# A mixer projection formed from seven block products instead of eight, with its input blocks kept on chip

## The chip, the cores and the metric

The kernel runs on one core of one Trainium2 chip. The metric is device time in microseconds (us), the median of several runs. The engines are named as the profile names them: PE (matrix products; PEld is its weight load), DVE (vector), ACT (scalar), POOL (GpSimd) and SP (which issues most DMAs here). Each engine runs its own instructions in a fixed order and waits at semaphores for the others.

## The reference

One decoder block over 1024 tokens of width 1024, in float32. What matters here is the middle of it:

```python
out_a = glu_a * jax.nn.sigmoid(glu_b)                  # from the state-space branch
out_b = att @ w_fox_o[l]                               # from the attention branch
gate_a, gate_b = jnp.split(jax.nn.sigmoid(gate_logits), 2, axis=-1)
h = h + (gate_a * out_a + gate_b * out_b) @ w_mix_out[l]
h = h + memory_cross_attention(rms_norm(h, norm_mem_q[l]), ..., w_mem_q[l], ...)
f_a, f_b = jnp.split(rms_norm(h, norm_ffn[l]) @ w_ffn_in[l], 2, axis=-1)
h = h + (jax.nn.silu(f_a) * f_b) @ w_ffn_out[l]
```

The mixer projection is the product with `w_mix_out` (1024 x 1024). The block `gate_a * out_a + gate_b * out_b` is called "merged" below.

## The kernel before

Every float32 operand is split into a high part (an fp32r cast, on ACT) and a low part (source minus high part, on DVE or POOL), by `split`. A product of two such operands is three matmuls: high by high, high by low, low by high. One matmul takes a 128 x 128 weight tile and 512 columns.

`stage_tail` holds everything from the gated unit on. Channels go in eight tiles of 128 (index `j`), tokens in eight tiles of 128 (`t`) or two halves of 512 (`h`).

- **The gated unit** (`Glu`): for each `j`, `value` and `sigmoid` form two products of 512 columns; DVE copies the first (L1239), ACT takes the sigmoid of the second into a half-width buffer `sb` (L1244), DVE multiplies them into the tile `sg` (L1245). `gate` then loads the gate `ga` from DRAM and multiplies `sg` by it on POOL (L1252), in two halves. The half-width buffers `sb`, `ga` and `gb` come from one small ring, so a new one waits for an older one's reader.
- **The attention branch** (`fox_part`): `po` is a product with `w_fox_o` (L173 to L175 with `ath`, `atl`) in a PSUM bank "pv" or "misc"; DVE multiplies it by the gate `gb` from DRAM (L616) and adds it to `sg` (L617). The merged tile is then split into `mxh`, `mxl` (`mT`).
- **The mixer** (`mix`): for each token tile and each half of the output, 8 channel tiles x 3 matmuls into one bank, then DVE adds a piece of `x` into `H[t]` (L668). The weights are `mix_weights`. Between the first twelve of these, `weave` puts the steps of `ahead(0)`, `ahead(1)`, `ahead(2)`, which prepare operands of the first three feed-forward tiles (`wpr`, `wph`, `wpl`) and store them to DRAM. The last four are followed by the norms of token tiles 0 to 3 (`norm`: a square on ACT, L190; a power on POOL, L211; small DVE steps L207 to L217; the scaled tile `xs` on DVE, L231; transposes on PE, L237; splits `u2h`, `u2l`).
- **The queries** (`mem_q`): products of `u2` with `w_mem_q`, with the norms of token tiles 4 to 7 between them.

The order on each engine is set by the build: a scheduler places the instructions by its own model within the order of the code, `B.behind(...)` and `issue_after` hold something back behind a named instruction, and pools of buffers (`wpool` with `whi`, `wlo` and four `raw`; `big` with bslot; `s2` with 16 slots; PSUM banks by tag) make a new tile wait for the last reader of an old one.

Of the kernel before, what the change touches and what calls it, by code (L numbers as in the profile page):

```python
# [9 lines left out]
F32 = mybir.dt.float32  # L10
F32R = mybir.dt.float32r
# [107 lines left out]
class Block:  # L119
# [126 lines left out]
    def norm_turn(self, xs, act, t):  # L246

        for b in range(2):
            cast = self.turned(self.turn(xs, b, ("misc", "pv")[b]), b, act, t)
        return cast  # L250
# [331 lines left out]
def stage_tail(B, big, s2, sh, x, glu, aT, gate_d, kv_d, w_fox_o, w_mix_out, g_mq, w_mem_q, w_mem_o, g_ffn,  # L582
# [18 lines left out]
    mT = Act(s2, "t", NS2, 8, L, name="mx")  # L601
    fox = {}

    def fox_part(j):
# [6 lines left out]
        for h in range(2):  # L611
# [5 lines left out]
            V.tensor_add(sg[:, cs], sg[:, cs], gb)  # L617
            mh, ml = mT.rhs(j, h)
            merged.append(B.split(mh, ml, sg[:, cs]))

    merged = []
    for j in range(8):
# [4 lines left out]
        glu.rest(j)  # L627
        if j > 2:
            fox_part(j - 3)
    for j in range(5, 8):  # L630
        fox_part(j)


    H = [bslot(name=f"h{t}") for t in range(NT)]
    gq = B.bcast_gain(s2, g_mq)
    u2 = Act(s2, "t", NS2, 8, L, name="u2")
# [6 lines left out]
    def wslots(src, pool_lo):  # L643

        nk = src.shape[0] // P
        raw = B.wpool.tile([P, RAW], F32, tag="raw", bufs=4, name="raw")[:, :D]
        S.dma_start(raw.rearrange("p (k c) -> p k c", k=nk), src.rearrange("(k p) c -> p k c", p=P))
        hl = bslot(F32R, "wbh"), bslot(F32R, "wbl")
        B.split(*hl, raw, pool_lo)
        return [t_.rearrange("p (k c) -> p k c", k=nk) for t_ in hl]  # L650

    def mix_weights(c):

        wm = ([], [])
        for kk in range(4):
            if c == 0:
                hl = B.wblock(w_mix_out, 2 * kk, 2, 0, 512)
            else:
                hl = wslots(w_mix_out[2 * kk * P:(2 * kk + 2) * P, 512:D], False)
            for w_, t_ in zip(wm, hl):  # L660
                w_ += [t_[:, 0, :], t_[:, 1, :]]
        return wm

    def mix(t, c, wm):
        cs = slice(512 * c, 512 * c + 512)
        ps = B.bank()
        gemm_n(ps, mT, t, wm, 8)
        V.tensor_add(H[t][:, cs], ps, load(x[t * P:(t + 1) * P, cs], "xr"))  # L668

    def norm(t, gb, act):  # L670
        xs = s2.tile([P, D], F32, tag="xs", bufs=1, name="xs")
        B.norm_scale(xs, H[t], B.rstd(H[t]), gb)
        return B.norm_turn(xs, act, t)
# [6 lines left out]
    def ahead(j):  # L680
# [14 lines left out]
        def plain():  # L695
            hl, _ = pair(0)
            with B.behind(merged[-1]):
                B.split(*hl, pre[j][0])
# [38 lines left out]
    with B.behind(merged[-1]):  # L737
        wm1 = mix_weights(1)
# [1252 lines left out]
```

## Time and profile before

| | |
|---|---|
| median of 3 runs | 1540.18 us (1540.08, 1540.18, 1541.64) |
| profiled execution, first to last instruction | 1538.1 us (its own time is not listed apart; the median lies 2.1 us above the span) |
| PE busy | 1520.7 us, 99% of the span, 7329 matmuls |
| DVE, ACT, POOL busy | 1005.7, 658.1, 253.6 us |
| granted PE clock | 0.999 |
| last sigmoid products and attention branch | up to 679.6 us |
| mixer products | 679.8 to 769.6 us |
| queries from | 770.6 us |

Times in the trace count from the span's first instruction. A row of the timeline gives the start, the length, the engine, the line, the operation and its tiles, how many instructions are merged in it, and in brackets the idle time before it with what ended it. A row of the stages gives for each engine its busy time and its number of instructions, then the granted PE clock, the share of the DMA engines that was busy, and their GB/s. A row of the groups gives the count, the busy total, the mean of one in ns, and the idle time before.

### The profile page before, as it was taken

The numbers are of one execution on the slowest core, as the hardware profiler recorded it, in microseconds if no ns is written. First come the engines' busy times: TensorE is split into PE (matmuls) and PEld (weight loads), VectorE is DVE, ScalarE is ACT, GpSimd is POOL, SyncE is SP. The second block draws the span as 40 slices with busy tenths as digits, with TensorE's granted clock in tenths as the row PEclk, the third lists the DMA queues.
The fourth block names the chain that finished last, engine by engine and source line by source line (L and its number), as shares of the span: only waits on it lengthen the run. The fifth ranks groups of instructions, "written<-read, shape, count | busy, mean of one in ns | idle before, by whom it ended". The sixth has DMA issues, their size and how long they took to land. (4 is left out here: it accounts for less than half of the span.)

```text
span 1538.1 us, 20434 instructions
## 1 busy us (share of the span) xinstructions
PE 1520.7 (99%) x7329; PEld 1257.7 (82%) x7329; DVE 1005.7 (65%) x1828; ACT 658.1 (43%) x1183; POOL 253.6 (16%) x341
## 2 busy tenths in 40 slices
PE   8999999999999999999999999999999999999998
PEld 7888888898777678888888888888888888888886
DVE  7936554355878867675556797777777775675555
ACT  7423334324667643232435663333333333354343
POOL 1166542100121214100102200000000000101001
PEclk9999999999999999999999999999999999999999
DMA  9634556611223746378210356555544544896542
GB/s 286 161 104 102 131 128 144 180 41 16 50 46 88 192 131 198 111 218 308 89 69 1 117 204 210 162 161 160 158 158 157 157 145 139 291 391 220 192 163 110
DMA packets 196293, 234.06 MB, mean 152 GB/s; under 512 B 35576, under 2 KB 127656, under 8 KB 195680
## 3 DMA queue, kind: packets, MB, share of 16 engines
q1 hardware_dynamic: 188704, 214.93, 47.0%
q10 hardware_dynamic: 7488, 17.83, 3.1%
q8 instruction: 57, 0.93, 0.3%
q14 instruction: 44, 0.36, 0.1%
HBM read 161.94 MB, written 72.71 MB: 153 GB/s over the span
## 5 line engine op out<-in xcount | busy, mean ns | idle before, releaser
L184 DVE TENSOR_TENSOR wlo<-raw,whi 128x1024 fp32r<-128x1024 f32 (+2 forms) x120 | 126.3, 1058 | 45.4 <-ACT whi L183 44.2
L183 ACT CAST whi<-raw 128x1024 fp32r<-128x1024 f32 (+2 forms) x120 | 108.7, 910 | 105.6 <-PE mm L174 39.1
L184 DVE TENSOR_TENSOR ol<-or,oh 128x1024 fp32r<-128x1024 f32 x73 | 90.1, 1236 | 74.0 <-ACT oh L183 71.9
L173 PE MATMUL mm<-uh,whi 128*128 128x512 f32 x344 | 136.5, 397 | 0.0
L174 PE MATMUL mm<-ul,whi 128*128 128x512 f32 x344 | 135.1, 393 | 0.0
L175 PE MATMUL mm<-uh,wlo 128*128 128x512 f32 x344 | 134.5, 391 | 0.0
L183 ACT CAST oh<-or 128x1024 fp32r<-128x1024 f32 x73 | 76.9, 1054 | 105.0 <-PE mm L1108 34.2
L997 POOL TENSOR_TENSOR g<-a,c 128x512 f32<-128x512 f32 x22 | 35.7, 1621 | 389.0 <-ACT a L996 389.0
L175 PEld LDWEIGHTS mm<-uh,wlo 128*128 128x128 f32 x344 | 64.7, 188 | 13.3 <-DVE wlo L184 0.2
L1803 POOL TENSOR_TENSOR pl<-pf,ph 128x512 fp32r<-128x512 f32 (+1 forms) x32 | 36.8, 1152 | 232.5 <-DVE ph L1802 193.3
L173 PEld LDWEIGHTS mm<-uh,whi 128*128 128x128 f32 x344 | 64.8, 188 | 11.6
L174 PEld LDWEIGHTS mm<-ul,whi 128*128 128x128 f32 x344 | 64.8, 188 | 11.0
L1800 ACT ACTIVATE pf<-sc 128x512 f32<-128x512 f32 (+1 forms) x96 | 46.4, 489 | 44.5 <-DVE sc L1796 28.3
L986 DVE SCALAR_TENSOR_TENSOR c<-c,pv 128x512 f32<-128x512 f32 x22 | 15.1, 687 | 76.5 <-ACT c L985 76.4
L211 POOL TENSOR_TENSOR r<-ms,mhalf 128x1 f32<-128x1 f32 (+1 forms) x26 | 15.7, 605 | 298.6 <-DVE ms L207 258.5
L964 PE MATMUL pv<-S3h,we 128*128 128x512 f32 x176 | 57.7, 389 | 0.0
L1806 DVE TENSOR_TENSOR pl<-pf,ph 128x512 fp32r<-128x512 f32 (+2 forms) x64 | 35.3, 553 | 10.4 <-ACT ph L1805 9.8
L1108 PE MATMUL mm<-ol,oh 128*128 128x512 f32 (+1 forms) x110 | 41.9, 381 | 0.0
L1108 PE MATMUL mm<-oh,ol 128*128 128x512 f32 (+1 forms) x110 | 41.9, 381 | 0.0
L1108 PE MATMUL mm<-oh 128*128 128x512 f32 (+1 forms) x110 | 41.9, 381 | 0.0
L173 PE MATMUL sc<-uh,whi 128*128 128x512 f32 x104 | 40.8, 392 | 0.0
L173 PE MATMUL mm<-yh,whi 128*128 128x512 f32 x104 | 40.7, 392 | 0.0
(639 smaller groups left out, 4554.2 us busy)
## 6 DMA issues: line engine op xcount, KB each, us to landing
or<-c_d SPq DMA_DIRECT2D x77, 256.0 KB
wo<-in_w_ffn_out_dram SPq DMA_DIRECT2D x22, 512.0 KB
c_d<-g SPq DMA_DIRECT2D x44, 256.0 KB
t_d<-wo SPq DMA_DIRECT2D x44, 256.0 KB
or<-t_d SPq DMA_DIRECT2D x44, 256.0 KB
rawb<-in_w_ffn_in_dram SPq DMA_DIRECT2D x20, 512.0 KB
raw<-in_w_ffn_in_dram SPq DMA_DIRECT2D x20, 512.0 KB
raw<-in_w_in_dram SPq DMA_DIRECT2D x19, 512.0 KB
```

Of the source, the lines that this page charges most:

```text
L173: T.matmul(ps, lh, rh, start=first, stop=False)
L174: T.matmul(ps, lh, rl, start=False, stop=False)
L175: return T.matmul(ps, ll, rh, start=False, stop=last)
L183: cast = self.A.copy(hi, src)
L184: self.rest = (self.G if pool_lo else self.V).tensor_sub(lo, src, f32(hi))
L211: self.G.tensor_tensor(out=r, in0=v, in1=self.mhalf[:, 0:n], op=ALU.pow)
L964: T.matmul(ps, l_[:, k, :], r_, start=first and k == 0 and i == 0, stop=k == 3 and i == 2, skip_group_check=True)
L997: G.tensor_mul(g[:, 512:], a1, c1)
L1108: T.matmul(ps, l_[:, gi], r_[:, c0:c1], start=k == 0 and (p == NP - LAST if own else p == 0 and n in (1, 2, 7)), stop=p == NP - 1 and k == ...
L1800: self.exp = A.activation(pf[:, off:], ps[:, off:], AF.Exp)
L1803: G.tensor_sub(pl[:, off:], pf[:, off:], f32(ph[:, off:]))
L1806: self.left = V.tensor_sub(pl[:, off:], pf[:, off:], f32(ph[:, off:]))
```

## The change

The mixer becomes seven products of 512-wide blocks (Winograd's form of Strassen's scheme): 7 products x 4 channel tiles x 4 token tiles x 3 matmuls, in place of 8 x 2 x 8 x 3.

- `fox_part` adds into block tiles (`block(n, p)`, kept on chip: `m1` to `m7`) instead of `sg`, and no longer splits; `merged_pair` makes four block combinations with four DVE instructions for each of four pairs.
- The weight combinations are made among the gated unit's steps: `mix_fetch` loads two weight tiles (`ws1`, `ws2`), `mix_sums` adds four halves on POOL, `mix_store` writes the four results to DRAM (`mt_d`). They are called for pairs 0 to 3 at `j` = 0 to 5.
- `m_get(m)` makes the operands of step `m` (28 steps, order `MORDER`): the weight half is loaded again, from `w_mix_out` or `mt_d`; ACT casts both halves, DVE makes the low part of the block half, POOL that of the weight half. Steps 0 to 3 use `whi`/`wlo`, later ones a ring of four pairs (`moh`, `mol`).
- `m_mm`, `m_step` and `m_add` do the products, in two sets of four banks, and add each finished product to `H`, which is now loaded with `x` first. Product 2 goes token tile by token tile (`m_tile`), product 3 follows; the norms of token tiles 0 to 3 are woven between them, both transposes in "pv" banks.
- `ahead(0)` is woven into steps 2 to 19; the steps of `ahead(1)` and `ahead(2)` are listed after them, among the last mixer steps and the queries; `plain` is no longer held behind the last merged tile.

```diff
-            V.tensor_add(sg[:, cs], sg[:, cs], gb)
-            mh, ml = mT.rhs(j, h)
-            merged.append(B.split(mh, ml, sg[:, cs]))
+            n = ((None, 1), (4, 2))[j % 2][h]
+            dst = block(n, j // 2) if n else sg[:, cs]
+            V.tensor_add(dst, sg[:, cs], gb)
...
+    def merged_pair(p):
+        a21 = gs.pop(p)
+        a11, a12, s1 = block(1, p), block(2, p), block(5, p)
+        V.tensor_sub(block(7, p), a11, a21)
+        V.tensor_sub(s1, block(4, p), a21)
+        V.scalar_tensor_tensor(out=block(6, p), in0=s1, scalar=-1.0, in1=a11, op0=ALU.mult, op1=ALU.subtract)
+        V.scalar_tensor_tensor(out=block(3, p), in0=block(6, p), scalar=-1.0, in1=a12, op0=ALU.mult, op1=ALU.subtract)
...
+    def mix_fetch(p):
+        msum[p] = slot(name="ws1"), slot(name="ws2")
+        for i, t_ in enumerate(msum[p]):
+            S.dma_start(t_, w_mix_out[(2 * p + i) * P:(2 * p + i + 1) * P, :])
+
+    def mix_sums(p):
+        w1, w2 = msum[p]
+        b11, b12, b21, b22 = w1[:, :512], w1[:, 512:], w2[:, :512], w2[:, 512:]
+        for o, i in ((b11, b12), (b12, b22), (b22, b11), (b21, b22)):
+            G.tensor_add(o, o, i)
+
+    def mix_store(p):
+        w1, w2 = msum.pop(p)
+        for n, o in ((5, w1[:, :512]), (7, w1[:, 512:]), (6, w2[:, 512:]), (4, w2[:, :512])):
+            S.dma_start(mt_d[n, p], o)
...
         glu.rest(j)
+        if j < 4:
+            mix_fetch(j)
+        if 0 < j < 5:
+            mix_sums(j - 1)
+        if 1 < j < 6:
+            mix_store(j - 2)
         if j > 2:
             fox_part(j - 3)
...
+    def m_get(m):
+        n, p = mseq[m]
+        rb = B.wpool.tile([P, RAW], F32, tag="raw", bufs=4, name="raw")[:, :512]
...
+        S.dma_start(rb, src)
+        if m < 4:
+            hl = [B.wpool.tile([P, WSLOT], F32R, tag=t_, name=t_)[:, :D] for t_ in ("whi", "wlo")]
+        else:
+            hl = bslot(F32R, "moh"), bslot(F32R, "mol")
+        B.split(hl[0][:, :512], hl[1][:, :512], mblk[n, p])
+        B.split(hl[0][:, 512:], hl[1][:, 512:], rb, True)
+        mops[m] = hl
+
+    def m_mm(m, i, ps):
+        n, p = mseq[m]
+        hi, lo = mops[m]
+        gi = slice(i * P, (i + 1) * P)
+        for k, (l_, r_) in enumerate(((hi, hi), (hi, lo), (lo, hi))):
+            T.matmul(ps, l_[:, gi], r_[:, 512:], start=k == 0 and p == 0 and n in (1, 2, 7),
+                     stop=p == 3 and k == 2, skip_group_check=True)
...
+        set_ = msets[n in (7, 4)]
+        for i in range(4):
+            m_mm(m, i, set_[i])
+        if p == 3:
+            for i in range(4):
+                m_add(n, i, set_[i])
+
+    def m_tile(i):
+        ps = B.bank(("mm", "misc")[i % 2])
+        for p in range(4):
+            m_mm(20 + p, i, ps)
+        m_add(2, i, ps)
...
+    weave([lambda m=m: m_next(m) for m in range(2, 20)], ahead(0), 4)
+    last = [lambda i=i: (m_tile(i), m_next(20 + i)) for i in range(4)] + [lambda m=m: m_step(m) for m in range(24, 28)]
+    fetched, *later = ahead(1) + ahead(2)
+    weave(last, [lambda t=t: norm(t, gq, u2, ("pv", "pv")) for t in range(4)] + [fetched])
```

How the instructions stand now is shown at three places. The first is POOL during the gated unit. `sg` tiles are multiplied by `ga` (the gates of `j` = 2 and 3 have `sg_5863` and `sg_5942`); `ws1`, `ws2` are the new weight sums. Before, the gates follow one another:

```order
L1252 TENSOR_TENSOR sg_5772<-sg_5772,ga_6087 128x512
L1252 TENSOR_TENSOR sg_5772<-sg_5772,ga_6090 128x512
L1252 TENSOR_TENSOR sg_5863<-sg_5863,ga_6125 128x512
L1252 TENSOR_TENSOR sg_5863<-sg_5863,ga_6128 128x512
L1252 TENSOR_TENSOR sg_5942<-sg_5942,ga_6163 128x512
```

Now, behind the gate of `j` = 1, twelve adds stand ahead of and between the gates of `j` = 2 and 3; the first four, of pair 0, stand ahead of these rows:

```order
L654 TENSOR_TENSOR ws1_6082<-ws1_6082 128x512
L654 TENSOR_TENSOR ws1_6082<-ws1_6082,ws2_6083 128x512
L654 TENSOR_TENSOR ws2_6083<-ws2_6083,ws1_6082 128x512
L1341 TENSOR_TENSOR sg_5863<-sg_5863,ga_6122 128x512
L654 TENSOR_TENSOR ws2_6083<-ws2_6083 128x512
L1341 TENSOR_TENSOR sg_5863<-sg_5863,ga_6125 128x512
L654 TENSOR_TENSOR ws1_6128<-ws1_6128 128x512
L654 TENSOR_TENSOR ws1_6128<-ws1_6128,ws2_6129 128x512
L654 TENSOR_TENSOR ws2_6129<-ws2_6129,ws1_6128 128x512
L654 TENSOR_TENSOR ws2_6129<-ws2_6129 128x512
L1341 TENSOR_TENSOR sg_5942<-sg_5942,ga_6172 128x512
```

Between the gates of `j` = 1 and `j` = 3 there were two instructions, the halves of the gate of `j` = 2; now there are fourteen.

The second is SP's queue at the same place, ahead of the first loads of `gb`. Before:

```order
L158 DMA raw_6629<-in_w_fox_o_dram 128x4x256
L222 DMA gbc_6801<-in_norm_mem_q_dram 128x1024
L1251 DMA ga_6163<-gate_d_79 128x512
L1251 DMA ga_6166<-gate_d_79 128x512
L597 DMA gb_6188<-gate_d_79 128x512
```

And now:

```order
L648 DMA ws1_6128<-in_w_mix_out_dram 128x1024
L648 DMA ws2_6129<-in_w_mix_out_dram 128x1024
L659 DMA mt_d_6001<-ws1_6040 128x512 x2
L659 DMA mt_d_6001<-ws2_6041 128x512 x2
L1340 DMA ga_6172<-gate_d_79 128x512
L1340 DMA ga_6175<-gate_d_79 128x512
L648 DMA ws1_6178<-in_w_mix_out_dram 128x1024
L648 DMA ws2_6179<-in_w_mix_out_dram 128x1024
L659 DMA mt_d_6001<-ws1_6082 128x512 x2
L659 DMA mt_d_6001<-ws2_6083 128x512 x2
L597 DMA gb_6209<-gate_d_79 128x512
```

The weight loads and the stores of the sums, which wait for POOL, have moved ahead of the loads that DVE's step L616 (now L617) needs.

The third is DVE at the mixer's end. Before, the last additions to `H` (L668) stand one at a time, each with one norm's steps behind it:

```order
L668 TENSOR_TENSOR h6_6799<-mm_7400,xr_7425 128x512
L184 TENSOR_TENSOR u2l0_0_6811<-misc_7441,u2h0_0_6803 128x2x128
L231 SCALAR_TENSOR_TENSOR xs_7487<-h3_6796,r01_7492,gbc_6801 128x1024
L184 TENSOR_TENSOR u2l1_0_6813<-misc_7441,u2h1_0_6805 128x2x128
L184 TENSOR_TENSOR u2l2_0_6815<-pv_7450,u2h2_0_6807 128x2x128
```

Now the last four (L710, of product 3) stand around the norm of tile 3, and splits of the query weights (`wlo`) behind them:

```order
L710 TENSOR_TENSOR h4_6706<-h4_6706,sc_6846 128x512
L216 SCALAR_TENSOR_TENSOR rt1_7577<-rt1_7577,ms1_7575 128x1
L184 TENSOR_TENSOR u2l3_0_6724<-pv_7538,u2h3_0_6716 128x2x128
L217 SCALAR_TENSOR_TENSOR r01_7576<-rt1_7577,r01_7576 128x1
L710 TENSOR_TENSOR h5_6707<-h5_6707,sc_6847 128x512
L231 SCALAR_TENSOR_TENSOR xs_7571<-h3_6705,r01_7576,gbc_6932 128x1024
L710 TENSOR_TENSOR h6_6708<-h6_6708,mm_6848 128x512
L710 TENSOR_TENSOR h7_6709<-h7_6709,mm_6849 128x512
L184 TENSOR_TENSOR u2l0_0_6718<-pv_7584,u2h0_0_6710 128x2x128
L184 TENSOR_TENSOR wlo_7645<-raw_7642,whi_7644 128x1024
```

`xs_7571`, which PE turns for the queries' operands, now follows two of the additions. The order also shows that the scheduler has put most of `ahead(1)` and `ahead(2)` on ACT and DVE among steps 15 to 20 of the mixer, earlier than the code lists them.

More of the change, by code (lines that the diff above doesn't have):

```diff
@@ L598, in load @@
         return t_
-    mT = Act(s2, "t", NS2, 8, L, name="mx")
-    fox = {}
+    fox, gs, done = {}, {}, {}
+    mt_d = B.dram.tile([8, 4, P, 512], F32, name="mt_d")
+    mblk = {}
     def fox_part(j):
@@ L641, in gemm_n, with norm @@
             B.mm3(ps, ah, al, w[0][k], w[1][k], k == 0, k == nk - 1)
[L643 to L670, printed above, removed]
+    def norm(t, gb, act, banks=("misc", "pv")):
         xs = s2.tile([P, D], F32, tag="xs", bufs=1, name="xs")
         B.norm_scale(xs, H[t], B.rstd(H[t]), gb)
-        return B.norm_turn(xs, act, t)
+        return B.norm_turn(xs, act, t, banks)
     AHEAD_IN = 2
```

77 lines of the change are left out of this document (59 added, 18 removed).

## The prediction

> **What bounds the kernel now.** I read the busy shares first, then the stages around the change, then PE's rows there, then POOL, DVE and SP in the gated unit. The shares (busy us, share, instructions):
>
> ```profile
> PE 1520.7 (99%) x7329; PEld 1257.7 (82%) x7329; DVE 1005.7 (65%) x1828; ACT 658.1 (43%) x1183; POOL 253.6 (16%) x341
> ```
>
> PE is the bound overall. The stages tell whether it also is where the change works:
>
> ```profile
> 590.00:595.00 5.00, 5.00 (x23) 4.14 (x23) 3.25 (x3) 1.75 (x3) 3.64 (x2) 1.00 0.95 282
> 595.00:600.00 5.00, 5.00 (x23) 4.13 (x22) 3.70 (x3) 0.28 (x1) 3.61 (x2) 1.00 0.86 309
> 600.00:605.00 5.00, 5.00 (x23) 4.13 (x22) 1.43 (x3) 0.62 (x1) 2.53 (x2) 1.00 0.85 257
> 679.00:723.00 44.00, 44.00 (x196) 36.44 (x195) 27.69 (x39) 14.74 (x21) 0.00 (x0) 1.00 0.84 278
> 723.00:770.00 47.00, 47.00 (x223) 39.16 (x222) 24.69 (x59) 18.64 (x45) 3.87 (x7) 1.00 0.36 126
> 770.00:802.00 32.00, 31.90 (x159) 26.31 (x158) 15.42 (x33) 11.16 (x28) 0.55 (x1) 1.00 0.22 83
> ```
>
> PE never waits in the mixer (679 to 770), and 0.10 us in the 32 behind it. So each matmul removed is worth its full pitch, and each new wait costs its full length. The reader should also see two things that are nearly full without being the bound: the DMA engines at 590 to 605 (0.85 to 0.95), and that POOL is idle in the mixer today.
>
> **The gain.** PE's rows give the pitch:
>
> ```profile
> 592.77 0.39 PE L173 MATMUL pv<-ath,whi 128*128 128x512 f32 x1
> 609.09 0.39 PE L173 MATMUL misc<-ath,whi 128*128 128x512 f32 x1
> 611.81 0.39 PE L173 MATMUL pv<-ath,whi 128*128 128x512 f32 x1
> ```
>
> From 609.09 to 611.81 are 12 matmuls: 2.72/12 = 0.2267 us each. The mixer had 8 x 2 x 8 x 3 = 384 and has 7 x 4 x 4 x 3 = 336. 48 fewer: **-10.9 us**. The transposes stay the same in number.
>
> **The gated unit.** Here the change adds POOL and DMA work. The rows:
>
> ```profile
> 590.83 3.64 POOL L1252 TENSOR_TENSOR sg<-sg,ga 128x512 f32<-128x512 f32 x2 [5.27 <-DMA ga<-gate_d]
> 596.10 3.61 POOL L1252 TENSOR_TENSOR sg<-sg,ga 128x512 f32<-128x512 f32 x2 [1.64 <-DMA ga<-gate_d]
> 600.13 2.53 POOL L1252 TENSOR_TENSOR sg<-sg,ga 128x512 f32<-128x512 f32 x2 [0.42 <-DMA ga<-gate_d]
> 612.71 3.01 POOL L1252 TENSOR_TENSOR sg<-sg,ga 128x512 f32<-128x512 f32 x2 [10.05 <-DVE sg L1245]
> 590.98 1.15 DVE L1245 TENSOR_TENSOR sg<-sg,sb 128x512 f32<-128x512 f32 x1
> 595.32 1.23 DVE L184 TENSOR_TENSOR wlo<-raw,whi 128x1024 fp32r<-128x1024 f32 x1
> 596.46 2.24 DVE L1245 TENSOR_TENSOR sg<-sg,sb 128x512 f32<-128x512 f32 x1
> 612.53 0.68 DVE L616 TENSOR_TENSOR gb<-gb,misc 128x512 f32<-128x512 f32 x1
> 613.25 1.32 DVE L617 TENSOR_TENSOR sg<-sg,gb 128x512 f32<-128x512 f32 x1
> 594.68 0.60 ACT L1244 ACTIVATE sb<-sc 128x512 f32<-128x512 f32 x1
> 587.81 1.07 SPq L1251 DMA_DIRECT2D ga<-gate_d x2
> DMA packets 3431, 4.24 MB, mean 283 GB/s; under 512 B 217, under 2 KB 2247, under 8 KB 3431
> ```
>
> (The last is the DMA view of 590 to 605.) POOL takes 2.53/2 = 1.265 us for a 128x512 operation when DVE is idle, and one beside a DVE instruction with two SBUF operands costs some 1.1 us more a pair (3.64, 3.61); DVE's own goes from 1.15 to 2.24, or from 0.68 to 1.32. A DVE instruction that reads PSUM (L616) stays at 0.68.
>
> The chain in the new order: `fox_part(1)`'s second half takes the "pv" bank that DVE frees by `gb x po` of `fox_part(0)`. On DVE that multiplication now stands behind the last sigmoid multiplication of `j` = 4, whose `sb` buffer is the `ga` that POOL reads in the first gate half of `j` = 3. Ahead of that half POOL has the twelve adds and the gate of `j` = 2: 15 operations counting itself, from 594.47 (590.83 + 3.64) on.
> - POOL: 15 x 1.265 = 19.0, to 613.5; five DVE instructions with two SBUF operands fall there, I count four at 1.08: to 617.8.
> - Then the sigmoid 0.60, the DVE multiplication beside POOL 2.24, `gb x po` 0.68: 621.3.
> - PE reaches that product at 611.81 + 6 x 0.2267 (six matmuls of the next product have been put ahead) = 613.2. **Wait 8.1 us.**
>
> Bounds: with no meeting 613.5 + 0.60 + 1.15 + 0.68 = 615.9, a wait of 2.7; with the cheapest POOL operation of that shape in the trace (below, 1.04) 15.6 us, and no wait: 0. All five meetings and 1 us for late loads give 10.3. I take 8.1, since the nearest rows are gates beside DVE. A second path ends there too: `gb` for that step now stands behind eight `ws` loads (4.2 MB) and eight stores (2.1 MB); with six gate halves, itself and one raw tile that makes 8.4 MB from 587.81 on, at 283 GB/s 29.6 us, to 617.4, and 0.68: a wait of 4.9 even if POOL were fast. Once PE is late, the later gates are in time: by the same prices pair 3's adds and the gate of `j` = 4 end by 630, their product is due at 638.
>
> **The mixer's steps.** Prices:
>
> ```profile
> L184 DVE TENSOR_TENSOR mxl<-sg,mxh 128x512 fp32r<-128x512 f32 x16 | 11.0, 688 | 2.8 <-ACT mxh L183 2.8
> L184 DVE TENSOR_TENSOR wpl<-wpr,wph 128x1024 fp32r<-128x1024 f32 x1 | 1.2, 1219 | 0.0
> 769.77 0.69 DVE L668 TENSOR_TENSOR h<-mm,xr 128x512 f32<-128x512 f32 x1 [1.68 <-PE mm L175]
> ```
>
> The removed `mxh`/`mxl` splits (16 each) and the sixteen pair combinations cancel on DVE; both lie beside PE, and cost nothing there. At step 4 PE needs the first bank read out by an addition that stands behind a 1.22 us split: 0 to 1.9 us, taken 0.7, since the split may have run.
>
> Steps 4 to 19 take PE 16 x 2.72 = 43.5 us, and PE reaches step 23's operands 9 matmuls later, 45.6. In that time DVE has, by the new order, 36 SBUF instructions at 0.688, one at 1.22 and 16 additions at 0.69: 37.0. POOL has 16 x 1.265 = 20.2, one after each step, where it had 0.00 and 3.87 in two stages. One meeting for each POOL operation at 1.32 - 0.69 = 0.63 makes DVE 47.1: **1.5 us late** at `m_tile(0)`. With no meeting 0; with one and a half for each 52.2, 6.6. I take the single meeting, as in the row at 613.25. The 4 MB of raw loads here replace the mixer's weights of like size; the stage 679 to 723 carried 278 GB/s without a wait of PE.
>
> [...]
>
> **The tail.** Norms 0 to 3 and product 3 are packed, and the norms of tiles 4 to 7 start later than before relative to PE:
>
> ```profile
> 764.22 0.63 ACT L190 ACTIVATE junk<-h 128x512 bf16<-128x512 f32 x1
> 766.47 0.20 DVE L207 TENSOR_SCALAR ms<-ss 128x1 f32<-128x1 f32 x1
> 766.75 0.55 POOL L211 TENSOR_TENSOR r<-ms,mhalf 128x1 f32<-128x1 f32 x1 [5.82 <-DVE ms L207]
> 767.75 0.15 DVE L216 SCALAR_TENSOR_TENSOR rt<-rt,ms 128x1 f32<-128x1 f32 x1
> 770.20 0.37 ACT L183 CAST u2h<-misc 128x256 fp32r<-128x256 f32 x1 [3.25 <-PE misc L237]
> 770.95 1.27 DVE L231 SCALAR_TENSOR_TENSOR xs<-h,r,gbc 128x1024 f32<-128x1024 f32 x1
> 772.14 0.42 DVE L184 TENSOR_TENSOR u2l<-misc,u2h 128x256 fp32r<-128x256 f32 x1
> 770.00 0.60 PE L237 MATMUL pv<-ident,xs 128*128 128x128 f32 x4
> ```
>
> - Product 3's first step uses the ring buffers that `m_tile(3)`'s early matmuls free, 10 matmuls (2.3 us) ahead; two casts and POOL's 1.265 need some 3.1 (casts taken as long as a square, 0.63 each, and hops): 0.8.
> - The turn of tile 2 needs, on DVE from `m_tile(2)`'s end on, six additions and low parts (4.1), six `u2l` (2.5), the power 0.55, small steps 0.7 and `xs` 1.27: 9.1 without a gap, against 37 matmuls (8.4) and two turns (1.2). With gaps for casts 0 to 1.4: 0.7.
> - The turn of tile 3 waits for `xs`, which stands behind two additions: 0.69 + 0.69 + 1.27 and hops and small steps 0.7, against the 9 matmuls left, 2.0: 1.3.
> - The turn of tile 4 follows two additions (1.38), four `u2l` (1.68), two `wlo` (2.46), three `ms` (0.60), the power 0.55, small steps 0.5, `xs` 1.27: 8.4, against two turns (1.2) and 28 matmuls (6.3): 0.9.
>
> Together **3.7 us**; 1.5 if the first two are covered by casts done early and the rest by half, 6 if each meets POOL. In the kernel before each addition of 0.69 stood alone, so none of these waits showed at 770 to 802.
>
> **The sum.** -10.9 + 8.1 + 0.7 + 1.5 + 3.7 = +3.1. The profiled span of 1538.1 becomes 1541.2; the median lies 2.1 above the span (1540.18), so **1543.3 us**.
>
> **The rivals.**
> 1. *The gates are not late.* Place: POOL from 594.47 on. If its adds cost what the nearest other 128x512 POOL operation costs, the chain ends before PE comes:
>
> ```profile
> L782 POOL TENSOR_TENSOR pe<-pe,sm x16: 1039/1040/2107, 807.1 to 865.6; 128x512 f32<-128x512 f32 x16
> ```
>
> At 1.04 us the wait is 0 and the time 1543.3 - 8.1 = 1535.2, faster. It turns faster (by 3.1 us) where the wait is below 1.9, so at up to 1.21 us for each operation. Against it: `sm` is spread from a narrower operand, the gates never went under 1.265, and the loads would need 340 GB/s.
>
> 2. *DVE and POOL take full turns in the steps.* Place: steps 4 to 23. Price: 37.0 + 20.2 = 57.2 us less what the additions (which read PSUM) cover, at most 10.1; halfway 52.2, 6.6 late instead of 1.5, and 1.3 more in the gated unit (5.9 us for five meetings in place of 4.3, less the shorter multiplication behind them): 1549.7. It decides once a step loses over 0.54 us ((45.6 - 37.0)/16). For it: the pair at 590.83. Against: the pair at 612.71, and that additions come four in a row. [...]
>
> 3. *The tail is hidden*: the scheduler's spread of the steps suffices, and 3.7 goes: 1539.6. For it: 31.90 of 32 us busy today with the same norms. Against: the order of the additions.
>
> **Chances.** A measurement of this kernel tells about 0.2%, 3.1 us, from no change. The forecast has 0.49: 0.28 slower, 0.21 within, as it lies on that bound. Rival 1 has 0.26 (0.22 faster, 0.04 within), rival 2 0.14 (slower), rival 3 0.11 (0.09 within, 0.02 faster). Faster 0.24, same 0.34, slower 0.42. The forecast's own range is 1538 to 1548; to leave out no more than 0.2 I go to 1533 (rival 1 with a tail of 1.5) and 1551 (past rival 2's time).
>
> **What would show it.** Right: PE waits once for 5 to 10 us near 613, released by DVE's L617, POOL's gates there 8 us or more behind; the steps' pitch stays 2.72 us; a wait of 1 to 2 us at `m_tile(0)`; 3 to 5 us of small waits from the first turn to the fifth. Wrong: no PE wait at 613 (rival 1), waits within steps 8 to 23 (rival 2), or a wait for a load of `mt_d`, which I put at nothing because the stores stand in SP's queue ahead of the gates of `j` = 5, and the first load of `mt_d` behind those of `j` = 6.

## The result, and the profile after

The changed kernel takes 1554.59 us (median of four, 1552.49 to 1555.81) against 1540.66 us for the kernel before on the same chip: a ratio of 1.0089, 95% interval 1.0075 to 1.0103. It is 14 us slower where 3 were forecast, and outside the range given (1533 to 1551).

The busy shares after. PE has the 48 matmuls fewer and yet a smaller share of a longer span; POOL and DVE have 65 and 38 us more.

```profile
PE 1518.3 (98%) x7281; PEld 1251.6 (81%) x7281; DVE 1043.6 (67%) x1860; ACT 670.3 (43%) x1215; POOL 318.4 (20%) x385
```

Nearly all of the loss lies between 613 and 800 us. The first matmul of the feed-forward stage, in the kernel before and then in the changed one, starts 15.2 us later:

```profile
899.46 0.47 PE L964 MATMUL mm<-A11h,wh 128*128 128x512 f32 x1
```

```profile
914.63 0.48 PE L1054 MATMUL mm<-A11h,wh 128*128 128x512 f32 x1
```

PE's long waits in that stretch, from the timeline of the changed kernel (in brackets the idle time and what ended it); of the five waits of the tail only the one above a microsecond is shown:

```profile
621.55 0.80 PE L173 MATMUL pv<-ath,whi 128*128 128x512 f32 x1 [8.01 <-DVE gb L617]
705.12 0.47 PE L703 MATMUL sc<-moh 128*128 128x512 f32 x1 [2.75 <-DVE h L710]
753.38 0.58 PE L703 MATMUL mm<-moh 128*128 128x512 f32 x1 [2.89 <-DVE h L710]
783.13 1.06 PE L237 MATMUL pv<-ident,xs 128*128 128x128 f32 x8 [1.11 <-DVE xs L231]
```

These are the four places that the prediction named. What it had no term for stands in the rows behind the first wait:

```profile
622.57 0.63 PE L175 MATMUL pv<-ath,wlo 128*128 128x512 f32 x1
623.00 0.63 PE L173 MATMUL pv<-ath,whi 128*128 128x512 f32 x1
627.76 0.40 PE L173 MATMUL mm<-yh,whi 128*128 128x512 f32 x1
627.99 0.39 PE L174 MATMUL mm<-yl,whi 128*128 128x512 f32 x1
```

Matmuls start 0.43 us apart for 5 us, then 0.23 again. In the stages (the column after the engines is the granted clock) it reads:

```profile
615.00:620.00 5.00, 0.00 (x0) 0.00 (x0) 0.52 (x1) 0.60 (x1) 4.92 (x4) 0.71 0.02 6
620.00:625.00 5.00, 3.45 (x8) 2.78 (x9) 4.37 (x5) 0.00 (x0) 4.84 (x4) 0.50 0.76 272
625.00:630.00 5.00, 5.00 (x18) 3.97 (x18) 2.53 (x2) 0.00 (x0) 4.28 (x4) 0.77 0.40 121
...
705.00:710.00 5.00, 4.88 (x15) 3.88 (x16) 4.27 (x7) 0.21 (x1) 0.00 (x0) 0.66 0.20 76
```

The granted clock is 0.71 from 615 to 620, while PE waits, and 0.50 from 620 to 625; matmuls stay 0.43 us apart until 627.27. The same follows the waits at 705 (the last row, rows of 0.63 us from 705.95 to 708.51) and 753 (0.80 from 755 to 760, rows of 0.63 us from 753.76 to 756.32). Summed over the rows, the time that matmuls started later than the full pitch is 2.8, 1.5 and 1.7 us behind the three waits: 6.0 us. (Some of the expectations below call such a stretch a slow window.)

The account, in us, by the trace of one execution:

| term | predicted | measured |
|---|---|---|
| 48 matmuls | -10.9 | -10.9 |
| gated unit | +8.1 | +8.2 |
| step 4 | +0.7 | +2.9 |
| `m_tile(0)` | +1.5 | +3.05 |
| tail | +3.7 | +3.9 |
| half clock behind the waits | none | +6.0 |
| other small gaps | none | +2.0 (what is left of the sum) |
| sum | +3.1 | +15.2 |

(The measured waits are differences of starting times less the pitch, 0.16 us above the figures in brackets. The -10.9 is the 48 matmuls fewer in the trace at the pitch of 0.2267 us.)

### The profile page after: what moved, and what is told of

It reads as the page before. It is cut to its first block, busy times and chain, and to the rows that moved or that the text cites. A ratio compares the mean times of both kernels' runs of the same rounds, so it can differ in the third digit from the quotient of the medians.

```text
span 1553.4 us, 20548 instructions
## 1 busy us (share of the span) xinstructions
PE 1518.3 (98%) x7281; PEld 1251.6 (81%) x7281; DVE 1043.6 (67%) x1860; ACT 670.3 (43%) x1215; POOL 318.4 (20%) x385
## 4 chain that ended last, share of the span: by engine, by line
PE 84%; DVE 7%; DMA 3%; ACT 2%; issue 2%; POOL 2%; SPq 0%; POOLq 0%; ACTq 0%; DVEq 0%
PE mm L1054 15%; PE pv L1054 8%; PE mm L173 7%; PE mm L175 7%; PE mm L174 7%; PE mm L1197 5%; PE sc L1054 4%; PE sc L1197 4%; PE pv L1197 3%; PE sc L175 3%; PE sc L174 3%; PE sc L173 3%; PE misc L1197 2%; PE mm L703 1%; PE sc L1882 1%
## 5 line engine op out<-in xcount | busy, mean ns | idle before, releaser
L184 DVE TENSOR_TENSOR wlo<-raw,whi 128x1024 fp32r<-128x1024 f32 (+2 forms) x116 | 121.7, 1055 | 40.4 <-ACT whi L183 39.3
L184 POOL TENSOR_TENSOR mol<-raw,moh 128x512 fp32r<-128x512 f32 x24 | 37.1, 1558 | 43.2 <-ACT moh L183 30.3
```

Of the source, the lines that this page charges most:

```text
L184: self.rest = (self.G if pool_lo else self.V).tensor_sub(lo, src, f32(hi))
```

## The experiments

Diffs are against the changed kernel unless said otherwise. Times stand beside those of the kernel before in the same session.

### The clock

**Matmuls in the wait.** 40 matmuls whose result nobody reads go into the wait near 613:

```diff
+            if j == h == 1:
+                fill = B.bank("sc")
+                for i in range(40):
+                    T.matmul(fill, fh[:, 0, o:o + P], aT.rhs(0, 0)[0], start=True, stop=True)
```

> Forty matmuls of 128x512 whose result nobody reads (9.1 us) are put on PE ahead of the attention product that waits at 613; that product cannot start before 621.5 as before. Theory (the clock is halved because PE stood idle): the granted clock stays at 1.00 between 610 and 630, the matmuls from 621.5 on have the pitch 0.227 us instead of 0.427, and since six useful matmuls now come behind the wait instead of ahead of it only 1.5 us of the 2.8 show: 1553 us. Rival (the slow matmuls come from what POOL, DVE and the DMAs do there): the pitch behind 621.5 stays 0.427 and the time rises by 1.4 us or more, 1556 us.

Measured 1561.46 us (before 1539.89; 1.0136, 1.0119 to 1.0152). The stages of this kernel:

```profile
615.00:620.00 5.00, 5.00 (x23) 4.14 (x23) 1.04 (x1) 0.60 (x1) 4.92 (x5) 1.00 0.00 0
620.00:625.00 5.00, 4.96 (x22) 3.75 (x21) 3.98 (x5) 0.00 (x0) 4.84 (x3) 1.00 0.87 306
```

And PE's rows behind the fill:

```profile
621.71 0.40 PE L175 MATMUL pv<-ath,wlo 128*128 128x512 f32 x1
638.74 0.79 PE L173 MATMUL mm<-yh,whi 128*128 128x512 f32 x1 [6.41 <-DVE sg L1332]
```

The product comes as late as before (621), but the clock stays at 1.00 and a matmul's row at 0.40 (0.63 in the changed kernel at that place). That part of the expectation holds: with PE at work the clock did not fall, though POOL beside it was as busy as in the changed kernel (4.92 and 4.84 us of each 5). The time does not follow, since a new wait of 6.4 us appeared at 638, with slow matmuls behind it (the row of 0.79). PE waits there for DVE's copy (L1332, from 637.61 us on), which this build puts behind a split at 635.87 us; that split waits 2.36 us for the cast of a weight tile whose load was issued at 630.28 us, behind the last four stores of the sums. In the changed kernel the copy stands ahead of that split and starts at 633.78 us. So the kernel is not the changed one with a busier PE alone: the order on DVE moved as well.

**Waits of set length.** In the kernel before, six pauses in the feed-forward stage:

```diff
+    pauses, held = {4: 4, 7: 6, 10: 8, 13: 10, 16: 14, 19: 20}, []
+        for i in range(k):
+            G.tensor_sub(zr, f32(zr), f32(zr))
+        held.append(T.matmul(pz[:, :P], zr, zr, start=True, stop=True))
```

> The kernel before, with six pauses put into the feed-forward stage, where PE otherwise never waits: in each a small unused product waits for a chain of POOL subtractions, longer from one to the next (4, 6, 8, 10, 14 and 20 of them). It measures by itself how long a wait of PE has to be for the granted clock to fall. [...] Time: 1540.7 plus the six waits and, by A, some 2 us for each that is long enough.

One execution: 1588.97 us. The waits came out as 1.93, 3.06, 4.58, 5.62, 7.45 and 10.82 us. The first and the last of them, then the stages with the clock at and behind these two:

```profile
981.36 0.33 PE L966 MATMUL misc<-zr 128*128 128x128 f32 x1 [1.93 <-POOL zr L964]
...
1309.92 0.47 PE L966 MATMUL misc<-zr 128*128 128x128 f32 x1 [10.82 <-POOL zr L964]
```

```profile
980.00:985.00 5.00, 3.64 (x10) 2.88 (x11) 2.54 (x4) 1.25 (x2) 1.15 (x3) 0.66 0.01 3
...
1310.00:1315.00 5.00, 5.00 (x12) 3.95 (x13) 0.00 (x0) 0.00 (x0) 0.00 (x0) 0.50 0.01 3
```

Each of the six halved the clock, the shortest too. The slow matmuls behind them cost 1.6, 1.3, 1.9, 1.8, 2.5 and 2.9 us. So a wait by itself is enough, which is the A of the expectation, and one of 1.93 us was enough here, less than the 2.75 and 2.89 us at step 4 and `m_tile(0)` of the changed kernel; the 2 us for each were the author's estimate. Over all PE waits of 1.2 us or more in the traces of this study, those up to 1.90 us left the clock alone, those from 4.0 us on all halved it, and of 29 between (1.93 to 3.21 us) 23 did; waits of 2.76, 2.77 and 3.21 us are among the six that did not. What decides between waits of one length was not shown.

### The gated unit

The chain of the prediction, in the changed kernel (POOL, ACT, DVE):

```profile
613.04 3.23 POOL L654 TENSOR_TENSOR ws<-ws,ws 128x512 f32<-128x512 f32 x2
616.34 1.26 POOL L654 TENSOR_TENSOR ws<-ws 128x512 f32<-128x512 f32 x1
617.56 2.48 POOL L1341 TENSOR_TENSOR sg<-sg,ga 128x512 f32<-128x512 f32 x2
618.85 0.60 ACT L1333 ACTIVATE sb<-sc 128x512 f32<-128x512 f32 x1 [7.50 <-POOL sg L1341]
619.48 1.50 DVE L1334 TENSOR_TENSOR sg<-sg,sb 128x512 f32<-128x512 f32 x1 [5.56 <-ACT sb L1333]
620.82 1.27 DVE L617 TENSOR_TENSOR gb<-gb,pv 128x512 f32<-128x512 f32 x2
```

POOL's gate of `j` = 3 stands behind the adds of pair 2; its first half frees the buffer that ACT waits for, DVE follows, then PE. Five kernels ask what of the new work makes it late.

**No adds.** The sixteen adds are left out; loads and stores stay.

```diff
-        for o, i in ((b11, b12), (b12, b22), (b22, b11), (b21, b22)):
+        for o, i in ():
```

> Leaves out the sixteen POOL additions that form the weight sums (products 4 to 7 then use plain weight blocks); the loads and stores of those tiles stay. [...] Rival (the loads of gb are late behind the new loads and stores): a PE wait of 4 us or more stays at 613 with half clock behind it, 1549 us or more.

1545.0 us (before 1539.89; 1.0032, 1.0021 to 1.0043), where 1542 to 1545 was expected: the changed kernel's time less some 11 us, the wait and the slow matmuls behind it. PE's wait there is 1.0 us, with no slow matmul behind it:

```profile
614.50 0.50 PE L173 MATMUL pv<-ath,whi 128*128 128x512 f32 x1 [1.00 <-DVE gb L617]
```

That is 9.6 us off the changed kernel's time: 7.0 of the wait and 2.8 of half clock. The adds set this wait, by POOL's time or by the stores that wait for them; the bytes alone do not.

**The sums later, and earlier.** Two kernels with the same work in another place: all of it three steps later; and pairs 0 and 1 ahead of the loop, pairs 2 and 3 at `j` = 4 to 6.

```diff
+        if 2 < j < 7:
+            mix_fetch(j - 3)
+        if 3 < j:
+            mix_sums(j - 4)
+            mix_store(j - 4)
```

> The weight sums are fetched, added and stored for pair p at j = p + 3 and p + 4, behind the gates that were late, with nothing left out. Theory: as with the additions left out, 1543.5 us (1542 to 1546), PE without a wait at 613, and the waits at 702, 750 and in the norms as in the changed kernel. Rival (the same DMA and POOL work makes later gates late instead): a wait of 3 us or more at another attention product between 613 and 690, 1549 us or more.

```diff
+    for p in range(2):
+        mix_fetch(p)
+    for p in range(2):
+        mix_sums(p)
...
+        if j in (5, 6):
+            mix_sums(j - 3)
...
+        if j > 3:
+            mix_store(j - 4)
+        if j in (4, 5):
+            mix_fetch(j - 2)
```

> The same work as the changed kernel; only the place of the weight sums differs: those of pairs 0 and 1 are fetched and added before the gated unit's loop, those of pairs 2 and 3 at j = 4 to 6, behind the gates that were late, and the stores stand behind each attention step. Theory (the adds ahead of the gates of j = 2 and 3 make the wait, and the wait halves the clock behind it): the wait of 8.2 us near 613 falls below 2 us and its slow stretch of 2.8 us goes; the waits of 2.9 us at step 4 and m_tile(0) stay, each with one slow window: 1554.6 - 8.2 - 2.8 + 1 = 1544.6 (1544 to 1546), as without the adds at all. Rival (the extra 6 MB of loads and stores in SP's queue make it, as they did when the sums were moved later): a wait of 5 to 8 us stays or moves to the next attention step, 1549 or more.

1552.3 us (before 1539.89; 1.0082, 1.0067 to 1.0097) and 1552.31 us (before 1539.94; 1.0082, 1.0068 to 1.0095): the rivals were right. The wait had moved to the next sigmoid product, as long as before and with slow matmuls behind it. In the kernel with the earlier sums, PE's row (0.79 us long, as the 0.80 behind the wait in the changed kernel), DVE's and two of SP's queue:

```profile
631.33 0.79 PE L173 MATMUL mm<-yh,whi 128*128 128x512 f32 x1 [7.80 <-DVE sg L1332]
625.01 0.69 DVE L617 TENSOR_TENSOR gb<-gb,misc 128x512 f32<-128x512 f32 x1 [8.17 <-DMA gb<-gate_d]
607.48 5.19 SPq L659 DMA_DIRECT2D mt_d<-ws  x8
616.78 2.63 SPq L597 DMA_DIRECT2D gb<-gate_d  x2
```

Here all eight stores stand in SP's queue ahead of the gate loads, and the load that DVE waits for lands 8 us after its issue. The kernel without the adds moves the same bytes and waits 1.0 us, so what counts here is the place of the stores in the queue.

**Out of the gated unit.** Loads, adds and stores in the state-space stage (with two `raw` tiles as buffers); or, beside the two moves at step 4 (below), in the attention stage, 256 columns at a time in one spare tile.

```diff
+    for p in range(4):
+        for k, g in ((2, mix_fetch), (5, mix_sums), (8, mix_store)):
+            todo.setdefault(k + 7 * p, []).append(lambda g=g, p=p: g(p))
```

> The changed kernel, with the weight sums, their loads and their stores moved out of the gated unit into the state-space stage some 300 us earlier, where POOL and the DMA engines were a fifth to a half busy. Theory (all of the wait near 613 and the half clock behind it come from the sums being made there, by POOL's adds or by their 6 MB of transfers; which of the two does not matter here): no wait of PE above 1 us from 560 to 700, no slow window there: 1554.6 - 8.2 - 2.8 = 1543.6 (1542.5 to 1545). Rival (POOL, the raw buffers or SP's queue are as tight in the state-space stage): new waits there, 1548 or more.

```diff
+                if 0 < h < 5 and n_ % 6 in (0, 2, 4):
+                    side[n_].append(lambda f=self.mix[n_ % 6 // 2], q=2 * h - 2 + n_ // 6: f(q))
```

> The two moves at step 4, and the weight sums made in the attention stage, at 340 to 400 us, in pieces of 128 x 256 in one spare tile; POOL stood idle there for 82 us and the DMA engines moved less than 50 GB/s. Theory (the sums cost PE nothing where POOL, the DMA engines and their buffers are free; the gated unit's wait of 7.2 us and its 2.8 us of half clock go): 1549.2 - 7.2 - 2.8 = 1539.2 (1538 to 1541), no different from the kernel before; what is left against the 48 matmuls (-10.9) are some 2.4 us at m_tile(0), 4.3 us in the tail and 3 to 4 us of small ones. Rival (as in the state-space stage, something there is tight: DVE beside POOL, or SP's queue ahead of the row maxima): new waits between 340 and 420 us, 1543 or more.

1560.9 us (before 1539.31; 1.0138, 1.0124 to 1.0152) and 1555.51 us (before 1540.39; 1.0102, 1.0084 to 1.0121). Both free the gated unit entirely: no wait of PE above 0.5 us from 560 to 700. And both pay elsewhere; PE's rows in the first kernel:

```profile
202.08 0.79 PE L175 MATMUL mm<-uh,wlo 128*128 128x512 f32 x1 [4.04 <-DVE wlo L184]
276.35 1.01 PE L1606 MATMUL pv<-xg,F 128*128 128x128 f32 x3 [6.96 <-ACT F L1567]
```

In the second:

```profile
369.24 0.50 PE L1867 MATMUL sc<-hb 69*128 69x512 f32 x1 [1.37 <-DMA hb<-mr]
390.27 0.69 PE L1837 MATMUL mm<-hb,hb 68*128 68x384 f32 x1 [2.70 <-DVE mc L1842]
```

An engine that is idle in a stage is not a free place: the weight loads behind two held `raw` tiles came late, and in the attention stage the row maxima (`hb<-mr`) stood in SP's queue behind the stores. That accounts for the wait at 369 us; the three of 2.4 to 2.7 us from 390 to 426 us, ended by DVE or ACT, were not traced further.

**The adds on DVE.** The same places, another engine:

```diff
-            G.tensor_add(o, o, i)
+            V.tensor_add(o, o, i)
```

> The changed kernel, with one letter changed: the sixteen adds of the weight sums run on DVE instead of POOL; loads, stores and their places in the code stay. DVE was busy 8.4 of the 15 us from 590 to 605 before, and takes 0.69 us where POOL takes 1.27. Theory (POOL's late gates make the wait near 613): the gates are in time, the wait falls to 1.5 us or less as without the adds, no slow window there: 1554.6 - 7 - 2.8 = 1544.8 (1543.5 to 1546.5). Rival (the transfers make it, or DVE now waits for the weight loads ahead of the work that PE needs): a wait above 4 us stays between 600 and 640, 1549 or more.

1550.78 us (before 1540.3; 1.0066, 1.0053 to 1.0078): 3.8 us better, where 10 were expected. The wait became 5.4 us. The build put all sixteen adds ahead of the multiplication that PE waits for. DVE first waits 3.1 and 0.6 us for the weight loads and then works without a wait from 596.8 us until that multiplication at 619 us. So the rival's second half was right (DVE is late, with the adds and the wait for their loads ahead of PE's work), as the rows of the next kernel show best. With the two moves at step 4 as well it is the next kernel:

> The adds on DVE and the two moves at step 4 together. Theory (costs add): 1549.2 - 7 - 2.8 = 1539.4 (1538 to 1541.5), no different from the kernel before: what then stands against the 48 matmuls (-10.9) is a wait of 1 us in the gated unit, 2.4 at m_tile(0), 4.3 in the tail and some 3 of small ones, all of them DVE's. Rival (as above): 1543 or more.

1547.37 us (before 1540.3; 1.0045, 1.0032 to 1.0057), with a wait of 5.1 us there; one of the twelve rows with adds, from 594 to 614, the multiplication and PE:

```profile
611.98 1.42 DVE L654 TENSOR_TENSOR ws<-ws,ws 128x512 f32<-128x512 f32 x2
617.14 1.27 DVE L617 TENSOR_TENSOR gb<-gb,pv 128x512 f32<-128x512 f32 x2
617.87 0.80 PE L173 MATMUL pv<-ath,whi 128*128 128x512 f32 x1 [5.08 <-DVE gb L617]
```

### Step 4

DVE in the changed kernel ahead of the first finished product's additions, and the POOL row beside it:

```profile
693.88 6.41 POOL L184 TENSOR_TENSOR mol<-raw,moh 128x512 fp32r<-128x512 f32 x4 [7.62 <-ACT moh L183]
695.65 1.79 DVE L620 TENSOR_TENSOR m<-sg,gb 128x512 f32<-128x512 f32 x1
...
699.06 1.78 DVE L639 TENSOR_TENSOR m<-m,sg 128x512 f32<-128x512 f32 x1
...
702.56 1.21 DVE L184 TENSOR_TENSOR wpl<-wpr,wph 128x1024 fp32r<-128x1024 f32 x1
704.30 1.27 DVE L710 TENSOR_TENSOR h<-h,sc 128x512 f32<-128x512 f32 x2
```

Three instructions take 1.78 us in place of 0.69 beside POOL's four low parts, and a split of 1.21 stands ahead of the additions. The next kernel takes both away:

```diff
-        B.split(hl[0][:, 512:], hl[1][:, 512:], rb, True)
+        B.split(hl[0][:, 512:], hl[1][:, 512:], rb, not 3 < m < 8)
...
+    def held(f):
+        with B.behind(adds[1][-1]):
+            f()
+
+    weave([lambda m=m: m_next(m) for m in range(4, 20)], [lambda f=f: held(f) for f in early[1:]], 2)
```

> The changed kernel, with two moves at the first finished mixer product: the low parts of the weight halves of steps 4 to 7 are made on DVE instead of POOL, so that POOL does not work beside DVE's last combinations, and the first feed-forward tile's splits are held behind the product's additions. Theory (DVE at double length beside POOL, and a 1.2 us split ahead of the additions, make the wait at step 4; without them DVE's four late instructions take 0.69 instead of 1.78 us): the wait of 2.9 us falls to 1 us or less, the slow window behind it goes: 1554.6 - 2 - 1.8 = 1550.8 (1550 to 1552). Rival (holding the splits back makes DVE later at m_tile(0), or the four more low parts cost DVE as much as they save): the wait stays above 2 us or the one at m_tile(0) grows, 1553 or more.

1549.23 us (before 1539.31; 1.0058, 1.0045 to 1.0072), 5.4 us off the changed kernel's time, and better than expected. The wait at step 4 is gone, although DVE makes four more low parts: without POOL beside it each of its instructions there takes 0.69 us. (The kernel with three moves under "Together" holds the splits alone, and its wait at step 4 is 2.35 us.) At `m_tile(0)` the wait shrank to 1.70 and its clock stayed whole:

```profile
746.55 0.47 PE L703 MATMUL mm<-moh 128*128 128x512 f32 x1 [1.70 <-DVE h L710]
```

```profile
742.00:747.00 5.00, 3.31 (x15) 2.48 (x14) 4.90 (x8) 3.16 (x6) 1.26 (x2) 1.00 0.49 194
```

### The last steps and the tail

In the changed kernel DVE comes to `m_tile(0)`'s addition late, with `ahead(1)`'s splits in front of it, of which two are shown merged, and idles twice for ACT's casts just before:

```profile
749.60 0.69 DVE L184 TENSOR_TENSOR mol<-m,moh 128x512 fp32r<-128x512 f32 x1 [0.78 <-ACT moh L183]
750.64 1.99 DVE L184 TENSOR_TENSOR wpl<-wpr,wph 128x512 fp32r<-128x512 f32 x2 [0.35 <-ACT wph L183]
752.56 0.68 DVE L710 TENSOR_TENSOR h<-h,mm 128x512 f32<-128x512 f32 x1
```

Two kernels hold the steps of `ahead(1)` and `ahead(2)` back, behind product 3's last addition or behind the last norm:

```diff
+            with B.behind(added[-1]):
+                f()
```

> All steps of ahead(1) and ahead(2) but the first loads are held behind the last addition of product 3. Theory: the wait of 3.05 us at the start of product 2 (PE for the additions to h, which stand behind two low parts of ahead(1) on DVE) goes, with 1.9 us of half clock behind it; the norms' waits stay within 1 us of 3.9: 1549.7 us (1548.5 to 1551.5). Rival (DVE and POOL sharing SBUF over steps 8 to 19 makes DVE late there whatever stands in its queue): a wait of 2 us or more stays, 1553 us or more.

```diff
+    with B.behind(normed[-1]):
+        for f in later:
+            f()
```

> The changed kernel, except that the operands of the second and third feed-forward tiles are made behind the last norm of the queries, so that none of their splits stands among the mixer's last steps or the norms. Theory (those splits on DVE are what product 2's first tile waits for, and the wait costs a slow window besides): the wait of 2.9 us at m_tile(0) falls below 1 us, the slow window behind it goes, the tail's small waits fall from 3.9 to about 3: 1554.6 - 2.4 - 1.8 - 0.9 = 1549.5 (1548.5 to 1551). Rival (the work only moves to another place where PE waits for it, as it did when it was held behind product 3): no gain, 1553 or more, with new waits behind 800 us.

1553.95 us (before 1539.89; 1.0091, 1.0071 to 1.0111), no different from the changed kernel, and 1564.22 us (before 1539.94; 1.0161, 1.0147 to 1.0174), 10 us worse. In both the wait at `m_tile(0)` fell below 0.9 us, so the first half of the theory holds, and the time came back elsewhere. The first kernel's largest new wait:

```profile
771.80 0.96 PE L237 MATMUL pv<-ident,xs 128*128 128x128 f32 x7 [3.21 <-DVE u2l L184]
```

The second kernel's:

```profile
826.76 0.80 PE L173 MATMUL mm<-u2h,whi 128*128 128x512 f32 x1 [8.24 <-ACT pe L872]
```

Why there is no room, the stages show: DVE, busy 24.69 of 47 us in the second half of the mixer before, is now busy 39.22 of 44. Changed kernel:

```profile
740.00:784.00 44.00, 38.51 (x175) 30.31 (x173) 39.22 (x67) 29.18 (x66) 18.07 (x14) 0.96 0.63 203
```

What is taken from one place on DVE is missing at the next.

### Together

Earlier sums (as in the second kernel of the gated unit), step 4's splits held, and the later operands behind the last norm:

> Three moves of work together, the same arithmetic as the changed kernel: the weight sums early (as in the run with that alone), the first feed-forward tile's splits behind the first finished mixer product's additions, and those of the second and third tiles behind the last norm. Theory (PE's waits and the half clock behind them are all that stands between the 48 matmuls saved and the time): of 26.1 us of waits and slow matmuls about 1 at the gated unit, 1 at step 4, 1 at m_tile(0) and 3 to 4 in the tail stay, no slow window: 1540.7 - 10.9 + 6.5 = 1536.3 (1534 to 1539), faster than the kernel before. Rival (waits reappear where the work was put, each above 2.5 us with its slow window): 1543 or more.

1564.0 us (before 1539.94; 1.0157, 1.0143 to 1.017). The rival: the waits of 8 us at 631 and at 827 return, each from its own part.

The sums in the state-space stage with both moves at step 4:

> The two together: the weight sums in the state-space stage, and the two moves at step 4. Theory (the costs add): 1554.6 - 11.0 - 3.8 = 1539.8 (1538.5 to 1541.5), what is left against 48 matmuls saved being the wait and slow window at m_tile(0), some 4.7 us, and the tail's 3.9: no slower than the kernel before. Rival (as with the moves of the feed-forward operands, the waits return elsewhere): 1543 or more.

1559.0 us (before 1539.31; 1.0124, 1.011 to 1.0138). The moves bring 1.9 of the 3.8 us expected, and the waits of the state-space stage stay.

The adds on DVE, the moves at step 4, and the adds of pairs 2 and 3 behind the second and third attention part:

```diff
+        if j in (4, 5):
+            with B.behind(last_add[0]):
+                mix_sums(j - 2)
+        if j in (6, 7):
+            mix_store(j - 4)
```

> The adds on DVE and the moves at step 4, with the adds of pairs 2 and 3 held behind the second and third attention part and their stores at j = 6 and 7. Theory (the adds cost PE nothing on an engine with room, as soon as none stands ahead of what PE waits for): eight adds of 0.69 fewer ahead of the first attention part, its wait falls from 5.2 to 1 us or less, no slow window: 1547.4 - 4.4 - 2.6 = 1540.4 (1539 to 1542.5), no different from the kernel before. Rival (the stores in SP's queue delay the gate loads again, as when the sums were moved later on POOL): a wait of 4 us or more near 630 to 650, 1545 or more.

1541.66 us (eleven runs, 1539.65 to 1543.71; before 1540.17; 1.0009, 1.0001 to 1.0018), within the expected 1539 to 1542.5. The wait near 613 is 1.84 us (1 or less was expected), the clock there stays whole, step 4 has no wait, and the mean clock is 0.999 as before the change:

```profile
616.44 0.50 PE L173 MATMUL pv<-ath,whi 128*128 128x512 f32 x1 [1.84 <-DVE gb L619]
740.00 0.47 PE L710 MATMUL mm<-moh 128*128 128x512 f32 x1 [1.58 <-ACT moh L183]
771.21 0.96 PE L237 MATMUL pv<-ident,xs 128*128 128x128 f32 x7 [1.42 <-DVE xs L231]
```

```profile
614.00:620.00 6.00, 4.16 (x18) 3.10 (x17) 5.02 (x7) 0.70 (x1) 3.00 (x2) 1.00 0.70 231
...
740.00:786.00 46.00, 41.60 (x196) 32.10 (x197) 40.57 (x84) 29.51 (x74) 15.40 (x15) 1.00 0.57 184
```

This brings back 12.4 of the 13.9 us with the arithmetic of the change whole. From the first attention product to the first matmul of the feed-forward stage the kernel before takes 306.7 us, the changed one 321.6 and this one 308.0. So waits and slow matmuls cost 25.8 us more than before in the changed kernel and 12.2 here, slightly more than the 10.9 that the 48 matmuls save. That DVE, busy 40.57 of 46 us at the end, holds what is left is not shown for all of it: of the five largest waits from 740 us to the queries three end by DVE, one by ACT (above) and one by POOL.

The same, with the query weights' splits held behind product 3:

```diff
-    wq = [B.wblock(w_mem_q, 0, 8, h * P, P) for h in range(MH)]
+    wq = [B.wblock(w_mem_q, 0, 8, h * P, P, behind=adds[3][-1] if h else None) for h in range(MH)]
```

> The same, and the splits of the query weights of all heads but the first held behind product 3's last addition. Theory (the wait of 1.6 us ahead of the turn of tile 3 is DVE doing three splits of 1.22 us ahead of xs): that wait falls to 0.5 us or less and the tail from 4.3 to 3.2: 1539.3 (1538 to 1541.5). Rival (the splits are then late for the queries): a new wait at the second query product, no gain.

1541.67 us (eleven runs; before 1540.17; 1.0013, 1.0004 to 1.0022). The wait of 1.42 us ahead of tile 3's turn is gone from its profile, one of 0.76 us ahead of tile 4's is new, and the time is the same within the intervals. No version tried beats the kernel before.

## Why the prediction was wrong, point by point

- **The gain and the chain of the gated unit: right.** 48 matmuls at 0.2267; PE came at 621.55 where 621.3 was worked out, a wait of 8.2 for 8.1, for the stated reason (no adds: 1.0 us). That the sum is so close is in part luck: POOL was 1 us later than thought and the DVE multiplication shorter (1.50 for 2.24). Rival 1, 0.26 of the chances, is out.
- **The second path there, a wait of 4.9 us by the transfers alone: wrong.** The kernel without the adds moves the same bytes and waits 1.0 us. The prediction took 283 GB/s as what the DMA engines can do. They moved 397 from 595 to 600:

```profile
595.00:600.00 5.00, 5.00 (x23) 4.13 (x22) 4.26 (x3) 0.60 (x1) 3.67 (x3) 1.00 1.02 397
```

- **Step 4, 0.7 us in bounds of 0 to 1.9: wrong.** It measured 2.9, above the bound, since that counted the split ahead of the additions and not that DVE's instructions before it would be beside POOL's low parts. Taking both away removed the whole wait.
- **`m_tile(0)`, 1.5 us in bounds of 0 to 6.6: mis-sized, and the path was another.** It measured 3.05. The sum had DVE at work without a pause and late by its load. From the first product's additions (704.30) to the one at 752.56 the number of instructions was about right (51 for 53). The meetings with POOL came to 9.9 us, by luck near the 16 x 0.63 = 10.1 of the sum: eleven of them, at up to 1.11 us each, so rival 2's price of one meeting was the nearer one, though its waits within steps 8 to 23 did not come. But back to back DVE's instructions start 0.60 us apart, not 0.69, and DVE idled 5.4 us, mostly for ACT's casts. What made PE wait is the order: the last matmul into the bank starts at 748.06 and DVE idles from 748.82 to 749.60, but the addition that empties the bank stands behind two splits of `ahead(1)`. With the steps of `ahead(1)` held back the wait fell below 0.9 us. Full turns over all the steps, as rival 2 has them, are shown by no run. But the pair at 590.83 (3.64 us for POOL's two operations, near 2.53 + 1.15 = 3.68) and the rows of step 4 (1.78 us for 0.69) are closer to them than the single meeting that I took.
- **The tail, 3.7 us: right in size** (3.9 in five waits of 0.6 to 1.3). Three stand where the prediction had them (0.6 us for 0.8 at product 3's first step, 1.3 for 1.3 at the turn of tile 3, 0.7 for 0.9 at that of tile 4). The other two, 0.7 and 0.6 us in the turns of tiles 1 and 2, wait for the low parts `u2l`, and not for `xs` as the 0.7 of the sum did. Rival 3 is out.
- **The step that failed most, a term that is missing: what a wait costs beyond its length.** The prediction says that "each new wait costs its full length". The three long waits cost 6.0 us on top of theirs, the largest part of the error of 12. The sum took PE at full clock, as it was in every stage of the kernel before that it shows. That kernel could show nothing else, as its PE, once started, has no wait above 1.24 us; the pauses put into it ("Waits of set length") show the same cost.

Of the error, 6.0 is the clock, 2.2 step 4, 1.6 `m_tile(0)`, 2.0 small gaps, 0.3 the rest. The doubts that I weighed (rivals 1 to 3) were about the size of known waits; the range had no room for a cost on top of them.

## What to carry to other kernels

Where PE is the bound at full clock, these traces price a new wait at its length and, from 1.93 us on, mostly at 1.3 to 2.9 us more for the slow matmuls behind it (23 of 29 waits up to 3.21 us, and all from 4.0 us on). Waits of up to 1.90 us left the clock whole here, so several short waits should be cheaper than one long one of the same sum. Work that is added to an engine with room is free only if nothing that PE waits for stands behind it in that engine's order, or in the queue that its transfers use: the same sixteen adds cost some 10 us on POOL among the gates, and left a wait of 1.84 us, against 1.00 without them, when they were spread on DVE. And before arithmetic is saved on the bounding engine, count what it adds to the second one (here DVE, from half to nine tenths busy at the mixer's end): the second one can take all of it back.

## What the hardware showed

- PE's clock fell to half in no wait up to 1.90 us, in 23 of 29 from 1.93 to 3.21, in all from 4.0 us on; the pitch of a 512-column matmul went from 0.227 to 0.427 us, mostly for 6 to 14 matmuls (1.3 to 2.9 us lost). With 40 unused matmuls in the wait near 613 the clock stayed at 1.00 from 615 to 625.
- A DVE instruction with two SBUF operands took 1.78 us beside a run of POOL's low parts and 0.69 alone; POOL's four took 6.41 us, 1.60 each, against 1.26 to 1.29 alone.
- The 16 DMA engines moved 397 GB/s over 5 us where the kernel before had shown 283 as a mean of a stretch in which they were 0.85 to 0.95 busy. Why the same engines moved more was not looked into.
